# The last branch's gates of a token mixer in pairs, as block products of seven instead of eight

## The chip, the cores and the metric

The kernel runs on one core of one Trainium2 chip. The metric is the device time of one execution in microseconds (us). PE is TensorE, the matrix engine; DVE is VectorE, ACT ScalarE, POOL GpSimd, and SP the engine whose queue issues all DMAs here. `before.py` took a median of 2324.22 us in 3 runs.

## The reference

Two layers, each with a feed-forward block, a mixer and a second feed-forward block, over 512 tokens of width 1024, all in float32. In the mixer the change touches the merge of three branches:

```python
proj = h @ w_in                      # 1024 -> 7184 columns, the last 3072 are gate logits
...
conv_out = conformer_conv(conv_in, ...)   # GLU, causal depthwise conv, LayerNorm over 512, swish
...
branches = jnp.stack([sb_out, conv_out, gla_out], axis=2)      # each 512 x 512
branch_d = jnp.einsum('bsgw,gwd->bsgd', branches, w_branch)    # each to width 1024
gates = jax.nn.sigmoid(gate_logits.reshape(b, s, N_BRANCHES, D_MODEL))
merged = jnp.sum(gates * branch_d, axis=2)
return merged @ w_out
```

## The kernel before

Activations lie with channels on the 128 partitions and the 512 tokens along the free dimension. A float32 product is made of three products in a reduced format: each operand is split into a high half (`whi`, `xh`: a cast on ACT) and a low half (`wlo`, `xl`: the value less its cast, on DVE), and PE sums high x high, high x low and low x high. The normalised input of a layer part is the pair `xh`, `xl`, 8 tiles of 128 channels each.

The feed-forward blocks compute gate and up columns of 128 together, in *block products* (`block_tiles`): the product of a 2 x 2 arrangement of weights (halves of the 1024 inputs, two column tiles) with a 2 x 2 arrangement of activations (halves of inputs, halves of tokens) takes 7 smaller products instead of 8, of sums of blocks. Such a unit has 7 products of 12 matmuls of 256 columns, into three PSUM banks A, B and C. The sums of the activation blocks (T1 to T4, `Forms`) are made once per block, those of the weight blocks per unit by `prepare`, on DVE; ACT copies partial results out of the banks (`taken`), DVE combines them (`summed`).

The mixer, function `mixer`, computes its gates in `gates(g, src, done)`, for one branch g at a time: for each of 8 column tiles d a gate product `gate` of 24 matmuls of 512 columns (L66, called from `mm_cols`), a sigmoid on ACT, a branch product `pb` of 12 matmuls with the split branch output, and the multiply of both on DVE (L1245) and the addition to `acc[d]` on POOL (L1246). The order of the branches is attention (g = 0), linear attention (g = 2), convolution (g = 1), the last. While the gates of branch 2 run, DVE finishes the convolution's taps and the layer norm: `ln_tokens(i)` transposes 128 tokens (`ct`), takes mean and variance and writes `yn[i]`; `ln_back(i)` transposes back into four banks `cb0` to `cb3`, one per channel tile, where each `yn[i]` fills a quarter. After u_ = 5 the four tiles are scaled, put through the swish (L1377 to L1379) and split (`brh`, `brl`), all before the last branch begins.

The output projection, `Down`, is a block product again over `acc[0]` to `acc[3]`; `acc[4]` to `acc[7]`, block rows 4 to 7 of `w_out`, come last as plain products (banks oC, oD, oB, oA). `Down.run` calls `late`, which loads the next two norm rows (`g`). Then the residual `x_sb` is added.

What sets the order: PE's instructions stand in the order of the code; operations marked `pinned` too; all others are moved by the framework's scheduler on their engine. Every engine takes its queue in order, so what waits holds up what stands behind it. Pools hand out buffers: the raw weight tiles have 3 of two 512 KB halves, `whi` and `wlo` 5 each, `g` 2, PSUM 2 banks in "pa" and 6 in "pb".

Of the kernel before, what the change touches and what calls it, by code (L numbers as in the profile page):

```python
# [13 lines left out]
P = 128  # L14
# [27 lines left out]
def kernel(  # L42
# [19 lines left out]
    sm = ctx.enter_context(tc.tile_pool(name="sm", bufs=4))  # L62
    psp = ctx.enter_context(tc.tile_pool(name="psp", bufs=1, space=PSUM))
# [335 lines left out]
    class Forms:  # L399
# [26 lines left out]

        def finish(self, n):
# [23 lines left out]
    def block_tiles(w0, w1, fs, forms, hid, between):  # L451
# [4 lines left out]
        silu = lambda o, i: pin(nc.scalar.activation(o, i, AF.Silu))  # L456
# [3 lines left out]
        n = 7 * len(fs)  # L460
        raw, banks, cps, ring = {}, {}, {}, {}

        def load(u):
            r = wp.tile([P, 5, 512], F32, tag="raw", name="raw", bufs=3)
            for w, q0 in ((w0, 0), (w1, 1)):
                for j in range(2):
                    nc.sync.dma_start(r[:, q0 + 2 * j].rearrange("p (k c) -> p k c", c=P),
                                      w[j * 512:(j + 1) * 512, fs[u] * P:(fs[u] + 1) * P]
                                      .rearrange("(k p) c -> p k c", p=P))
            raw[u] = r  # L470
# [46 lines left out]
        def parts(u):  # L517
            cp = cps[u]
            return [cp[:, x * 256:(x + 1) * 256] for x in range(4)], hid[fs[u]], banks[u]

        def taken(g):

            u, j = divmod(g, 7)
            (p1, p7, u2, u4), h, (A, B, C) = parts(u)
            if j == 0:
                copy(p1, A[:, H0])
            if j == 1:
                copy(p7, C[:, H0])
            if j == 2:
                copy(u2, A[:, H0])  # L530
            if j == 4:
                copy(u4, A[:, H0])
            if j == 6:
                silu(h[:, H0], h[:, H0])
                silu(h[:, H1], A[:, H0])

        def summed(g):

            u, j = divmod(g, 7)
            (p1, p7, u2, u4), h, (A, B, C) = parts(u)  # L540
            if j == 3:
                add(h[:, H0], B[:, H0], p1)
            if j == 5:
                sub(u2, C[:, H0], u2)
                sub(u4, p7, u4)
            if j == 6:
                tt(h, cps[u][:, 512:1024], h, ALU.mult)

        for g in range(-AHEAD, n + 1):
            between(g)  # L550
            f = g + AHEAD
            if f % 7 == 0 and f < n:
                if f == 0:
                    load(0)
                if f // 7 + 1 < len(fs):
                    load(f // 7 + 1)
# [14 lines left out]
    class Down:  # L571
# [66 lines left out]
        def sums(self, p):  # L638
# [162 lines left out]
    def ffn(wg, wu, wd, weights, forms, arrive, finish, upcoming, early, late, begin):  # L801
# [72 lines left out]
        block_tiles(wg, wu, fs, forms, hid, between)  # L874
# [4 lines left out]
    def mixer(l, wv, arrive, finish, upcoming, early, late):  # L879
# [24 lines left out]

        cw = mp.tile([P, 4, NR], F32, tag="cw", name="cw")
# [270 lines left out]
        for h in range(HEADS):  # L1176
# [9 lines left out]
            att_values(h, ws)  # L1186
        next(decay[0])
# [13 lines left out]
        def gate_weights(g, d):  # L1201
            return load_cols(W, C_GATE + g * D + d * P)

        def gate_branch(g, d, src, wb, w):
# [5 lines left out]
            wh, wl = wb  # L1210
# [5 lines left out]
            return pb, sg  # L1216
# [13 lines left out]
        def gates(g, src, done):  # L1230

            early_ = done is not None
            following = gate_weights(g, 0) if early_ else None
            for d in range(0, KC, 2):
                wb = load_branch(g, d)
                for dd in (d, d + 1):
                    w = following if early_ else gate_weights(g, dd)
                    if early_ and dd + 1 < KC:
                        following = gate_weights(g, dd + 1)
                    pb, sg = gate_branch(g, dd, src, wb[dd - d], w)  # L1240
# [6 lines left out]
                    if done is not None:  # L1247
                        done(dd)
                    yield

        sb_gates = gates(0, branch_split(sbT, "s"), None)
# [82 lines left out]
        gla_gates = gates(2, branch_split(glaT, "t"), None)  # L1334


        cb = []
# [16 lines left out]
        def ln_back(i):  # L1354
            if not cb:
                cb.extend(bank(f"cb{c}") for c in range(4))
            for c in range(4):
                transpose(cb[c][:, i * P:(i + 1) * P], yn[i][:, c * P:(c + 1) * P], ident)

        for u_ in range(KC):  # L1360
            next(gla_gates)
            conv_taps(10)
            if u_ == 3:
                ln_tokens(0)
                ln_tokens(1)
            if u_ == 4:
                ln_back(0)
                ln_back(1)
                ln_tokens(2)
                ln_tokens(3)  # L1370
            if u_ == 5:
                ln_back(2)
                ln_back(3)
                for c in range(4):
                    g_, b_ = cw[:, c, TAPS + 1:TAPS + 2], cw[:, c, TAPS + 2:TAPS + 3]
                    s_ = slot("cs", tag="s")
                    nc.scalar.activation(s_, cb[c], AF.Sigmoid, scale=g_, bias=b_)  # L1377
                    nc.vector.tensor_scalar(ys[c], cb[c], g_, b_, op0=ALU.mult, op1=ALU.add)
                    nc.vector.tensor_tensor(ys[c], ys[c], s_, op=ALU.mult)  # L1379
                cv = branch_split(ys, "s")  # L1380
# [3 lines left out]
        down.pairs()  # L1384

        def merge(d):
            for n in range(2):
                down.sum_tokens(d, n)
            if d == KC - 2:
                for n in range(3):  # L1390
                    down.ahead()
# [23 lines left out]
    for idx, (l, s) in enumerate(subs):  # L1415
        norms = []

        def late():
            norms.append(load_g(norm_post[l, s]))
            if idx + 1 < len(subs):  # L1420
# [61 lines left out]
```

## Time and profile before

| | |
|---|---|
| three runs | 2323.63, 2324.22, 2324.99 us |
| the profiled execution | 2321.75 us, of which the span of its instructions 2320.0 us |
| granted PE clock, mean | 0.999 |
| busy in the span | PE 99%, DVE 81%, ACT 53%, POOL 8% |
| DMA | 269 MB, 116 GB/s in the mean |
| gates and branch products on the chain that ended last | PE gate 11%, PE pb 6% of the span |

Views of the profile are the page with its groups of instructions, the list of who waited for whom, the chain of work that ended last in order of time, timelines of one engine, and busy times by stretch. A row of a timeline has start, length, engine, line, operation, output and inputs, number, and in brackets the idle time before it with its releaser. Matmuls are pipelined: the length of one is longer than the distance to the next.

### The profile page before, as it was taken

The numbers are of one execution on the slowest core, as the hardware profiler recorded it, in microseconds if no ns is written. First come the engines' busy times: TensorE is split into PE (matmuls) and PEld (weight loads), VectorE is DVE, ScalarE is ACT, GpSimd is POOL, SyncE is SP. The second block draws the span as 40 slices with busy tenths as digits, with TensorE's granted clock in tenths as the row PEclk, the third lists the DMA queues.
The fourth block names the chain that finished last, engine by engine and source line by source line (L and its number), as shares of the span: only waits on it lengthen the run. The fifth ranks groups of instructions, "written<-read, shape, count | busy, mean of one in ns | idle before, by whom it ended". The sixth has DMA issues, their size and how long they took to land.

```text
span 2320.0 us, 35537 instructions
## 1 busy us (share of the span) xinstructions
PE 2296.1 (99%) x13664; PEld 2031.0 (88%) x13664; DVE 1884.6 (81%) x2819; ACT 1240.6 (53%) x2414; POOL 177.2 (8%) x277
## 2 busy tenths in 40 slices
PE   8999999999999999999999999999999999999998
PEld 7999888887888889998889998888878888899987
DVE  7888987859965688889888889878599647888897
ACT  5555656644323565556555566566433225566664
POOL 0000001201021200000000000012010212000000
PEclk9999999999999999999999999999999999999999
DMA  5333643131333423336433336432313324333363
GB/s 174 100 101 110 229 153 102 55 103 49 110 91 106 140 73 103 99 109 235 147 87 97 108 110 235 150 88 62 97 55 105 96 91 136 91 98 104 114 222 109
DMA packets 336219, 269.49 MB, mean 116 GB/s; under 512 B 13130, under 2 KB 285548, under 8 KB 336048
## 3 DMA queue, kind: packets, MB, share of 16 engines
q1 hardware_dynamic: 336048, 267.21, 38.0%
q8 instruction: 107, 1.75, 0.3%
q14 instruction: 64, 0.52, 0.1%
HBM read 265.07 MB, written 2.10 MB: 115 GB/s over the span
## 4 chain that ended last, share of the span: by engine, by line
PE 96%; DVE 2%; ACT 1%; issue 0%; DMA 0%; POOL 0%; SPq 0%; DVEq 0%; POOLq 0%; ACTq 0%
PE A L66 19%; PE gate L66 11%; PE oA L66 10%; PE C L66 9%; PE oC L66 6%; PE pb L66 6%; PE B L66 5%; PE oB L66 3%; PE pf L66 3%; PE gr L66 2%; PE pa L66 2%; PE q L66 2%; PE gv L66 2%; PE pv L66 2%; PE pgl L66 2%; PE k L66 2%
## 5 line engine op out<-in xcount | busy, mean ns | idle before, releaser
L457 DVE TENSOR_TENSOR wlo<-raw,whi 128x1024 fp32r<-128x1024 f32 (+1 forms) x304 | 331.1, 1089 | 106.9 <-ACT whi L455 106.1
L455 ACT CAST whi<-raw 128x512 fp32r<-128x512 f32 x532 | 315.3, 620 | 164.7 <-DVE raw L457 164.7
L115 ACT CAST whi<-raw 128x1024 fp32r<-128x1024 f32 (+1 forms) x162 | 168.1, 1044 | 329.8 <-PE gate L66 143.6
L116 DVE TENSOR_TENSOR wlo<-raw,whi 128x1024 fp32r<-128x1024 f32 (+1 forms) x162 | 203.4, 1265 | 137.3 <-ACT whi L115 133.0
L457 DVE TENSOR_TENSOR raw<-raw 128x512 f32<-128x512 f32 x304 | 209.2, 688 | 5.7
L66 PE MATMUL A<-xh,whi 128*128 128x256 f32 x608 | 172.5, 284 | 0.0
L66 PE MATMUL A<-xh,wlo 128*128 128x256 f32 x608 | 172.0, 283 | 0.0
L66 PE MATMUL A<-xl,whi 128*128 128x256 f32 x608 | 172.0, 283 | 0.0
L1055 DVE SCALAR_TENSOR_TENSOR y<-u,cw,y 128x511 f32<-128x511 f32 (+14 forms) x240 | 166.7, 755 | 0.0
L686 DVE TENSOR_TENSOR wlo<-raw,whi 128x1024 fp32r<-128x1024 f32 x122 | 148.8, 1220 | 17.8 <-ACT whi L683 17.5
L683 ACT CAST whi<-raw 128x1024 fp32r<-128x1024 f32 x122 | 128.4, 1052 | 63.8 <-issue 20.8
L66 PE MATMUL gate<-xh,whi 128*128 128x512 f32 x384 | 151.3, 394 | 0.0
L66 PE MATMUL gate<-xh,wlo 128*128 128x512 f32 x384 | 149.8, 390 | 1.3 <-DVE wlo L116 1.3
L66 PE MATMUL gate<-xl,whi 128*128 128x512 f32 x384 | 149.6, 390 | 0.0
L66 PE MATMUL oA<-whi,dl 128*128 128x512 f32 x352 | 137.0, 389 | 0.0
L66 PE MATMUL oA<-whi,dh 128*128 128x512 f32 x352 | 137.0, 389 | 0.0
L66 PE MATMUL oA<-wlo,dh 128*128 128x512 f32 x352 | 136.9, 389 | 0.0
L268 POOL TENSOR_TENSOR rs<-ms,mhalf 128x1 f32<-128x1 f32 x44 | 25.1, 576 | 1415.2 <-DVE ms L266 1415.2
L455 ACT COPY cp<-A 128x256 f32<-128x256 f32 x228 | 84.4, 370 | 66.5 <-PE A L66 65.6
L66 PEld LDWEIGHTS A<-xl,whi 128*128 128x128 f32 x608 | 116.6, 192 | 0.2
L66 PEld LDWEIGHTS A<-xh,whi 128*128 128x128 f32 x608 | 116.5, 192 | 0.2
L66 PEld LDWEIGHTS A<-xh,wlo 128*128 128x128 f32 x608 | 116.5, 192 | 0.0
(330 smaller groups left out, 6947.4 us busy)
## 6 DMA issues: line engine op xcount, KB each, us to landing
raw<-in_ffn_w_down_dram SPq DMA_DIRECT2D x152, 512.0 KB, 4.5
raw<-in_w_in_dram SPq DMA_DIRECT2D x108, 512.0 KB, 4.7
raw<-in_ffn_w_gate_dram SPq DMA_DIRECT2D x168, 256.0 KB, 3.4
raw<-in_ffn_w_up_dram SPq DMA_DIRECT2D x168, 256.0 KB, 4.5
raw<-in_w_branch_dram SPq DMA_DIRECT2D x24, 512.0 KB, 4.8
raw<-in_w_out_dram SPq DMA_DIRECT2D x24, 512.0 KB, 4.9
g<-in_norm_pre_dram SPq DMA_DIRECT2D x6, 512.0 KB, 6.8
g<-in_norm_post_dram SPq DMA_DIRECT2D x6, 512.0 KB, 5.8
```

The source lines that it names most:

```text
L66: tc.keep_in_program_order(nc.tensor.matmul(*a, **k))
L115: pin(nc.scalar.copy(hi, src))
L116: pin(nc.vector.tensor_tensor(lo, src, hi.bitcast(F32), op=ALU.subtract))
L268: nc.gpsimd.tensor_tensor(self.rs, ms, mhalf[:, 0:1], op=ALU.pow)
L455: copy = lambda o, i: pin(nc.scalar.copy(o, i))
L457: tt = lambda o, a, b, op: pin(nc.vector.tensor_tensor(o, a, b, op=op))
L683: pinned(nc.scalar.copy(hi, src))
L686: pinned(nc.vector.tensor_tensor(lo, src, hi.bitcast(F32), op=ALU.subtract))
L1055: nc.vector.scalar_tensor_tensor(y[:, back:], u[:, :S - back], cw[:, c, j:j + 1], y[:, back:], op0=ALU.mult, op1=ALU.add)
```

## The change

The gates of the last branch (g = 1) are computed in pairs (d, d + 1) as block products, by the same `block_tiles` as the feed-forward part: 4 units of 7 products of 12 matmuls of 256 columns in place of 8 products of 24 matmuls of 512. `block_tiles` now takes its weights, its target and what is done with the result as functions; a unit is prepared from 4 products ahead. After each unit follow the two branch products of its pair, in banks of "pa".

What the units need and what moves for it:
- The sums T1 to T4 are rebuilt from `xh` and `xl` (`Forms.rebuild`): T1 and T2 ahead of `conv_in(1)`, T3 and T4 behind the gates u_ = 3 and 4 of branch 2.
- Room for T1 and T2: the four tiles of the residual `x_sb`. So x is stored to DRAM at the mixer's start (`away`, 4 x 512 KB per layer) and loaded again in `Down.run`, between the norm rows (`back`).
- `ln_back(c)` now makes one channel tile c from all four `yn`, in steps: transposes ahead of product c of the first unit, swish one product later, split another one later, on pinned places. The last two gates of branch 2 run at g = -2 and g = 0 of the units' counter, that is ahead of the first product.
- The gates of branch 2 ask for their weights 2 column tiles ahead.
- For the last pair the addition to `acc` is on DVE, not POOL. `Down` keeps one of its weight sums in the place of `xh` and not in a second `g` buffer.

```diff
-    def block_tiles(w0, w1, fs, forms, hid, between):
+    def block_tiles(source, count, forms, target, result, between, ahead=AHEAD, wait=0):
...
             if j == 6:
-                silu(h[:, H0], h[:, H0])
-                silu(h[:, H1], A[:, H0])
+                results[u] = result(u, h, A[:, H0], cps[u][:, 512:1024])
+                next(results[u])
...
+        def rebuild(self, c, room_, second):
...
+            r11 = tokens(0, 0)
+            if not second:
+                r12 = tokens(0, 256)
+                tt(r12, r11, r12, ALU.subtract)
+                keep("T1", r12)
+                r22 = tokens(4, 256)
+                nc.vector.scalar_tensor_tensor(r22, r12, -1.0, r22, op0=ALU.mult, op1=ALU.subtract)
+                keep("T2", r22)
+                return
+            t2 = whole(*room_("T2", c))
+            tt(r11, t2, r11, ALU.add)
+            keep("T3", r11)
+            r21 = tokens(4, 0)
+            tt(r21, t2, r21, ALU.add)
+            keep("T4", r21)
...
-                    self.apart = [gp.tile([P, D], F32, tag="g", name="kept") for n in range(2)]
+                    self.apart = [gp.tile([P, D], F32, tag="g", name="kept")]
+                elif self.PER == 1 and j == 3:
+                    self.kept = room("xh", F32)
+                    self.apart.append(self.place(0))
...
+        for i in range(NT):
+            nc.sync.dma_start(away[i], x_sb[i])
...
+        for c in range(2):
+            mforms.rebuild(c, form_room, False)
         next(decay[0])
         conv_in(1)
...
+        def ln_back(c):
+            cb = bank("cb", "pa")
+            for i in range(NT):
+                transpose(cb[:, i * P:(i + 1) * P], yn[i][:, c * P:(c + 1) * P], ident)
+            yield
+            g_, b_ = cw[:, c, TAPS + 1:TAPS + 2], cw[:, c, TAPS + 2:TAPS + 3]
+            s_ = slot("cs", tag="s")
+            pinned(nc.scalar.activation(s_, cb, AF.Sigmoid, scale=g_, bias=b_))
+            pinned(nc.vector.tensor_scalar(ys[c], cb, g_, b_, op0=ALU.mult, op1=ALU.add))
+            pinned(nc.vector.tensor_tensor(ys[c], ys[c], s_, op=ALU.mult))
+            yield
+            held[0] = True
+            cv.extend(branch_split([ys[c]], "s"))
+            held[0] = False
...
+        def merged(u):
+            if u > 0:
+                for d in (2 * u - 2, 2 * u - 1):
+                    for n in range(2):
+                        down.sum_tokens(d, n)
+            for m, (ps, sg) in enumerate(zip(pbs[u], made[u])):
+                pinned(nc.vector.tensor_tensor(sg, ps, sg, op=ALU.mult))
+                d = 2 * u + m
+                (nc.vector if u == PAIRS - 1 else nc.gpsimd).tensor_tensor(acc[d], acc[d], sg, op=ALU.add)
+
+        def between(g):
+            u, j = divmod(g, 7)
+            if g in (-2, 0):
+                next(gla_gates)
+            if u == 0:
+                if j < 4:
+                    backs.append(ln_back(j))
+                for b in backs[-3:]:
+                    next(b, None)
+            if 0 <= u < PAIRS and j == 2:
+                held[0] = True
+                wbs[u] = load_branch(1, 2 * u)
+                held[0] = False
+            if u > 0 and j == 0:
+                branch_products(u - 1)
+            if u > 0 and j == 1:
+                merged(u - 1)
+            if g in (7 * PAIRS - 2, 7 * PAIRS - 1, 7 * PAIRS):
+                down.ahead()
+
+        block_tiles(source, PAIRS, mforms, target, sigmoids, between, 4, 4)
+        merged(PAIRS - 1)
+
+        def back():
+            for i in range(NT):
+                if i % 2 == 0:
+                    late(i // 2)
+                x_sb[i] = resid.tile([P, D], F32, tag=f"x{i}", name=f"x{i}")
+                pinned(nc.sync.dma_start(x_sb[i], away[i]))
-        for _ in gates(1, cv, merge):
-            pass
-        head = down.run(late, ("B0", "B1", "C0", "C1", "D0", "D1"))
+        head = down.run(back, ("B0", "B1", "C0", "C1", "D0", "D1"))
```

The order of the instructions at three places of the first layer (the numbers behind the names are those of the tiles). First DVE's queue from the scaling of the four channel tiles to the last low half, before: `cb0` to `cb3` are the banks of the way back, `cs` their sigmoid, `brl` the low half of the branch output, `gs` a gate multiplied with its branch product.

```order
L1378 TENSOR_SCALAR y_5463<-cb0_6900,cw_4134 128x512
L1378 TENSOR_SCALAR y_5548<-cb1_6901,cw_4134 128x512
L1379 TENSOR_TENSOR y_5463<-y_5463,cs_6995 128x512
L1379 TENSOR_TENSOR y_5548<-y_5548,cs_6999 128x512
L1378 TENSOR_SCALAR y_5647<-cb2_6902,cw_4134 128x512
L1378 TENSOR_SCALAR y_5743<-cb3_6903,cw_4134 128x512
L1379 TENSOR_TENSOR y_5647<-y_5647,cs_7003 128x512
L1379 TENSOR_TENSOR y_5743<-y_5743,cs_7007 128x512
L116 TENSOR_TENSOR brl_7012<-y_5463,brh_7011 128x512
L116 TENSOR_TENSOR wlo_7142<-raw_7134,whi_7141 128x1024
L116 TENSOR_TENSOR brl_7016<-y_5548,brh_7015 128x512
L116 TENSOR_TENSOR brl_7020<-y_5647,brh_7019 128x512
```

Now, from the last gate multiply of branch 2 (`gs_7148`) on; `raw_7063` holds the weights of the first unit, `raw_7170` those of the second, `wlo_7235` is the low half of the branch weights:

```order
L1315 TENSOR_TENSOR gs_7148<-pb_7150,gs_7148 128x512
L1432 TENSOR_SCALAR y_5473<-cb_7165,cw_4144 128x512
L1433 TENSOR_TENSOR y_5473<-y_5473,cs_7194 128x512
L493 TENSOR_TENSOR raw_7063<-raw_7063 128x512
L493 TENSOR_TENSOR wlo_7192<-raw_7063,whi_7191 128x2x512
L117 TENSOR_TENSOR brl_7221<-y_5473,brh_7220 128x512
L1432 TENSOR_SCALAR y_5586<-cb_7198,cw_4144 128x512
L1433 TENSOR_TENSOR y_5586<-y_5586,cs_7224 128x512
L117 TENSOR_TENSOR wlo_7235<-raw_7014,whi_7234 128x1024
L493 TENSOR_TENSOR wlo_7252<-raw_7063,whi_7251 128x512
L117 TENSOR_TENSOR brl_7256<-y_5586,brh_7255 128x512
```

and on to the last low half:

```order
L1432 TENSOR_SCALAR y_5685<-cb_7228,cw_4144 128x512
L1433 TENSOR_TENSOR y_5685<-y_5685,cs_7259 128x512
L493 TENSOR_TENSOR raw_7170<-raw_7170 128x512 x2
L493 TENSOR_TENSOR wlo_7252<-raw_7170,whi_7251 128x512
L117 TENSOR_TENSOR brl_7291<-y_5685,brh_7290 128x512
L1432 TENSOR_SCALAR y_5781<-cb_7263,cw_4144 128x512
L1433 TENSOR_TENSOR y_5781<-y_5781,cs_7294 128x512
L493 TENSOR_TENSOR gs_7203<-B_7176,cp_7178 128x256
L117 TENSOR_TENSOR brl_7315<-y_5781,brh_7314 128x512
```

The four tiles' scaling, multiply and split moved from one block behind the second gate from the end of branch 2 to places between the first unit's weight sums and weight halves, behind the multiply of branch 2's last gate.

Second, PE's queue where the last branch uses its first split tiles. Before, the first branch product of the last branch, behind a gate product of 24 matmuls:

```order
L66 MATMUL pb_7172<-brh_7011,whi_7136 128x512
L66 MATMUL pb_7172<-brl_7012,whi_7136 128x512
L66 MATMUL pb_7172<-brh_7011,wlo_7137 128x512
L66 MATMUL pb_7172<-brh_7015,whi_7136 128x512
L66 MATMUL pb_7172<-brl_7016,whi_7136 128x512
L66 MATMUL pb_7172<-brh_7015,wlo_7137 128x512
```

Now the last matmuls of the first branch product, which stands directly behind the first unit; `brl_7315` is the last of DVE's rows above:

```order
L67 MATMUL pb_7351<-brh_7290,whi_7234 128x512
L67 MATMUL pb_7351<-brl_7291,whi_7234 128x512
L67 MATMUL pb_7351<-brh_7290,wlo_7235 128x512
L67 MATMUL pb_7351<-brh_7314,whi_7234 128x512
L67 MATMUL pb_7351<-brl_7315,whi_7234 128x512
L67 MATMUL pb_7351<-brh_7314,wlo_7235 128x512
```

The branch product moved from behind a whole gate product to behind the unit in which its operands are made.

Third, SP's queue in the output projection, before:

```order
L127 DMA raw_7638<-in_w_out_dram 128x1024
L127 DMA raw_7693<-in_w_out_dram 128x1024
L193 DMA g_7689<-in_norm_post_dram 128x1024
L127 DMA raw_7693<-in_w_out_dram 128x1024
L193 DMA g_7691<-in_norm_pre_dram 128x1024
L127 DMA raw_7750<-in_w_out_dram 128x1024
L127 DMA raw_7750<-in_ffn2_w_gate_dram 128x2x256
```

and now:

```order
L128 DMA raw_7952<-in_w_out_dram 128x1024
L128 DMA raw_8015<-in_w_out_dram 128x1024
L194 DMA g_8003<-in_norm_post_dram 128x1024
L1519 DMA x0_8005<-away0_4136 128x1024
L1519 DMA x1_8007<-away1_4137 128x1024
L194 DMA g_8009<-in_norm_pre_dram 128x1024
L1519 DMA x2_8011<-away2_4138 128x1024
L1519 DMA x3_8013<-away3_4139 128x1024
L128 DMA raw_8015<-in_w_out_dram 128x1024
L128 DMA raw_8072<-in_w_out_dram 128x1024
L128 DMA raw_8072<-in_ffn2_w_gate_dram 128x2x256
```

The four loads of x stand between the norm rows, ahead of block rows 6 and 7 of `w_out` (the last two `w_out` rows in each list), which stood behind one norm row each.

More of the change, by code (lines that the diff above doesn't have):

```diff
@@ L518, in parts @@
             cp = cps[u]
-            return [cp[:, x * 256:(x + 1) * 256] for x in range(4)], hid[fs[u]], banks[u]
+            return [cp[:, x * 256:(x + 1) * 256] for x in range(4)], target(u), banks[u]
         def taken(g):
@@ L546, in summed @@
             if j == 6:
-                tt(h, cps[u][:, 512:1024], h, ALU.mult)
-        for g in range(-AHEAD, n + 1):
+                next(results[u], None)
+        for g in range(-ahead, n + 1):
             between(g)
[L551 to L556, printed above, removed]
+            f = g + ahead
+            if f == 0:
+                load(0)
+            if f < n and (f == wait if f < 7 else f % 7 == 0) and f // 7 + 1 < count:
+                load(f // 7 + 1)
             if 0 < g:
@@ L873, in ffn, with source, gated @@
         down = Down(wd, hid, 2, 8, (0, 1), (18, 19, 20, 21))
-        block_tiles(wg, wu, fs, forms, hid, between)
+        def source(u):
+            return (wg, fs[u] * P), (wu, fs[u] * P)
+        def gated(u, h, a, second):
+            pinned(nc.scalar.activation(h[:, H0], h[:, H0], AF.Silu))
+            pinned(nc.scalar.activation(h[:, H1], a, AF.Silu))
+            yield
+            pinned(nc.vector.tensor_tensor(h, second, h, op=ALU.mult))
+        block_tiles(source, len(fs), forms, lambda u: hid[fs[u]], gated, between)
         head = down.run(late)
@@ L903, in mixer @@
             vcat.append(row)
+        away = [scr.tile([P, D], F32, tag=f"away{i}", name=f"away{i}") for i in range(NT)]
+        for i in range(NT):
+            nc.sync.dma_start(away[i], x_sb[i])
         cw = mp.tile([P, 4, NR], F32, tag="cw", name="cw")
@@ L1186, in mixer, with form_room @@
             att_values(h, ws)
+        mforms = Forms()
+        rooms = {}
+        def form_room(n, c):
+            if n not in rooms and n in ("T1", "T2"):
+                j = 0 if n == "T1" else 2
+                rooms[n] = [resid.tile([P, D], F32R, tag=f"x{j + m}", name=f"{n}{m}")
+                            .rearrange("p (k t) -> p k t", k=4) for m in range(2)]
+            if n in rooms:
+                return [r[:, 2 * c:2 * c + 2] for r in rooms[n]]
+            return [slot(n, F32R, "t" if n == "T3" else "b").rearrange("p (k t) -> p k t", k=2) for m in range(2)]
+        for c in range(2):
+            mforms.rebuild(c, form_room, False)
         next(decay[0])
@@ L1228, in branch_split, with gates, ask @@
             return r
-        def gates(g, src, done):
-            early_ = done is not None
-            following = gate_weights(g, 0) if early_ else None
+        def gates(g, src, ahead=0):
+            wb, w = {}, {}
+            def ask(d):
+                if d < KC and d not in w:
+                    if d % 2 == 0:
+                        wb[d], wb[d + 1] = load_branch(g, d)
+                    w[d] = load_cols(W, C_GATE + g * D + d * P)
             for d in range(0, KC, 2):
-                wb = load_branch(g, d)
                 for dd in (d, d + 1):
[L1237 to L1240, printed above, removed]
+                    ask(dd)
+                    for n in range(ahead):
+                        ask(dd + 1 + n)
+                    pb, sg = gate_branch(src, w.pop(dd), wb.pop(dd))
                     if acc[dd] is None:
@@ L1246, in gates @@
                         nc.gpsimd.tensor_tensor(acc[dd], acc[dd], sg, op=ALU.add)
-                    if done is not None:
-                        done(dd)
                     yield
-        sb_gates = gates(0, branch_split(sbT, "s"), None)
+        sb_gates = gates(0, branch_split(sbT, "s"))
         gnB = mp.tile([P, 512], F32, tag="row", name="gnB")
@@ L1352, in ln_tokens @@
             nc.vector.tensor_scalar(yn[i], pt, mv[:, 0:1], rs, op0=ALU.subtract, op1=ALU.mult)
[L1354 to L1360, printed above, removed]
+        cv = []
+        def ln_back(c):
[8 more added lines that the diff above has]
+            pinned(nc.vector.tensor_tensor(ys[c], ys[c], s_, op=ALU.mult))
+            yield
+            held[0] = True
+            cv.extend(branch_split([ys[c]], "s"))
+            held[0] = False
+        for u_ in range(KC - 2):
             next(gla_gates)
@@ L1365, in mixer @@
                 ln_tokens(1)
+            if u_ in (3, 4):
+                mforms.rebuild(u_ - 3, form_room, True)
             if u_ == 4:
-                ln_back(0)
-                ln_back(1)
                 ln_tokens(2)
                 ln_tokens(3)
[L1371 to L1380, printed above, removed]
@@ L1383, in mixer, with source @@
         down = Down(w_out[l], acc, 0, 2, (), (4, 5, 6, 7))
         down.pairs()
[L1386 to L1391, printed above, removed]
-        for _ in gates(1, cv, merge):
-            pass
-        head = down.run(late, ("B0", "B1", "C0", "C1", "D0", "D1"))
+        PAIRS = KC // 2
+        wbs, pbs, made, backs = {}, {}, {}, []
+        def source(u):
+            c0 = C_GATE + D + 2 * u * P
+            return (W, c0), (W, c0 + P)
@@ new lines, in target, with sigmoids, branch_products @@
+        def target(u):
+            if u not in made:
+                made[u] = [slot("gs", tag="s")]
+            return made[u][0]
+        def sigmoids(u, h, a, second):
+            pinned(nc.scalar.activation(h[:, H0], h[:, H0], AF.Sigmoid))
+            pinned(nc.scalar.activation(h[:, H1], a, AF.Sigmoid))
+            pinned(nc.scalar.activation(second, second, AF.Sigmoid))
+            made[u].append(second)
+            yield
+        def branch_products(u):
+            pbs[u] = [bank("pb", "pa") for m in range(2)]
+            for ps, (wh, wl) in zip(pbs[u], wbs[u]):
+                branch_product(ps, cv, wh, wl)
@@ L1416, with late @@
         norms = []
-        def late():
-            norms.append(load_g(norm_post[l, s]))
-            if idx + 1 < len(subs):
+        def late(*which):
+            if not which or 0 in which:
+                norms.append(load_g(norm_post[l, s]))
+            if idx + 1 < len(subs) and (not which or 1 in which):
                 norms.append(load_g(norm_pre[subs[idx + 1][0], subs[idx + 1][1]]))
```

35 lines of the change are left out of this document (22 added, 13 removed).

## The prediction

> **What bounds the kernel now.** I read the page's busy times and its chain first, then what TensorE (PE) waited for, then the chain in order of time through the first layer's mixer, and last VectorE's (DVE) and ScalarE's (ACT) queues at the places that the change touches.
>
> ```profile
> PE 2296.1 (99%) x13664; PEld 2031.0 (88%) x13664; DVE 1884.6 (81%) x2819; ACT 1240.6 (53%) x2414; POOL 177.2 (8%) x277
> PE 96%; DVE 2%; ACT 1%; issue 0%; DMA 0%; POOL 0%; SPq 0%; DVEq 0%; POOLq 0%; ACTq 0%
> ```
>
> PE is busy in 2296 of 2320 us and carries 96% of the chain. Its waits, the whole list (us in total, times, longest):
>
> ```profile
> PE pt L71 <- DVE hn L223: 7.5, 1, 7.5
> PE pf L66 <- ACT xh L115: 4.3, 4, 2.0
> PE pt L71 <- DVE hn L290: 3.0, 3, 1.0
> PE gate L66 <- DVE wlo L116: 1.3, 2, 0.6
> PE pf L66 <- DVE xl L116: 0.8, 4, 0.2
> ```
>
> The gates' two waits, 1.3 us together, lie ahead of the last branch, which has none, as the chain shows next; so no wait can be removed there. The change can gain only by giving PE less to do, and can lose by making PE wait. What PE does, from the chain in order of time (start, length, what), with the last branch of both layers, the output projection behind it, and one block product of the feed-forward part for comparison:
>
> ```profile
> 687.18 0.87 PE cb L71 x8
> 697.11 0.87 PE cb L71 x8
> ...
> 714.32 5.44 PE gate L66 x24
> 719.76 2.72 PE pb L66 x12
> ...
> 776.88 2.72 PE pb L66 x12
> 779.60 2.72 PE oB L66 x12
> ...
> 866.78 1.44 PE A L66 x12
> 868.22 1.44 PE C L66 x12
> ...
> 1866.05 5.44 PE gate L66 x24
> ...
> 1931.33 2.72 PE oB L66 x12
> ```
>
> The reader sees a stage without a gap: from 714.32 to 779.60 are 65.28 us, which is 8 x (5.44 + 2.72), and from 1866.05 to 1931.33 again 65.28. One product of 512 columns costs 5.44 / 24 = 0.2267 us of PE, one of 256 columns 1.44 / 12 = 0.1200 us. The durations in the groups must not be used for this, since neighbours overlap:
>
> ```profile
> L66 PE MATMUL A<-xh,whi 128*128 128x256 f32 x608 | 172.5, 284 | 0.0
> L66 PE MATMUL gate<-xh,whi 128*128 128x512 f32 x384 | 151.3, 394 | 0.0
> ```
>
> **The change part by part.** *PE work.* A layer loses 8 gate products of 24 and gets 4 units of 7 block products of 12 short ones: 8 x 5.44 = 43.52 us becomes 28 x 1.44 = 40.32 us, so -3.20 us. Branch products (8 x 2.72) and the 16 transposes of the way back (2 x 0.87) stay, only placed otherwise. Two layers: -6.40 us, all of it on the path.
>
> The Trainium skill (TensorE: Matmul & The Clock Gate, Back-to-back issue gap) gives N / 2.4 + 2.5 ns between warm matmuls, 109 and 216 ns here. By it a pair of gates would save 48 x 0.2158 - 84 x 0.1092 = 1.19 us, 9.5 us in all, and the time would be an estimated 2314.7. The trace has 120 and 227 ns, 11 ns more in each case, and decides.
>
> *The first unit's DVE chain, the only stall that I find.* Before, the layer norm's way back was done long ahead of its use. Now one channel tile after another is transposed inside the first unit, and the branch product right behind this unit needs all four. DVE's rows of that time before:
>
> ```profile
> 700.28 1.52 DVE L1378 TENSOR_SCALAR y<-cb,cw 128x512 f32<-128x512 f32 x2
> 701.72 1.27 DVE L1379 TENSOR_TENSOR y<-y,cs 128x512 f32<-128x512 f32 x2
> 702.92 1.52 DVE L1378 TENSOR_SCALAR y<-cb,cw 128x512 f32<-128x512 f32 x2
> 705.56 0.68 DVE L116 TENSOR_TENSOR brl<-y,brh 128x512 fp32r<-128x512 f32 x1
> 706.17 1.21 DVE L116 TENSOR_TENSOR wlo<-raw,whi 128x1024 fp32r<-128x1024 f32 x1
> 707.30 1.88 DVE L116 TENSOR_TENSOR brl<-y,brh 128x512 fp32r<-128x512 f32 x3
> 714.42 0.69 DVE L1245 TENSOR_TENSOR gs<-pb,gs 128x512 f32<-128x512 f32 x1 [0.66 <-PE pb L66]
> 705.07 1.28 ACT L115 CAST brh<-y 128x512 fp32r<-128x512 f32 x2 [0.21 <-DVE y L1379]
> ```
>
> From start to start a scaled read of PSUM takes 1.44 / 2 = 0.72 us, a 512-wide operation 0.60 to 0.61, a 1024-wide one 1.13. In the new order DVE stands at the last gate multiply (gs) of the branch ahead until that product ends; this and 19 more operations come ahead of the low half (brl) of the last channel tile: 4 scaled reads, 13 of 512 (gs, 4 multiplies, 3 weight sums, 3 brl, 2 single low halves of weights), 2 of 1024 and one of 256 at about 0.3. That is 4 x 0.72 + 13 x 0.61 + 2 x 1.13 + 0.3 = 13.4 us, with the last brl at its full 0.68 14.0; two waits for ACT come to it (about 0.3 for a cast that stands behind a bank copy, 0.4 for the last high half, a cast of 0.6 us that can't start before its multiply has ended): 14.7 us. PE: without the two 0.87 us of transposes the branch ahead ends at 714.32 - 1.74 = 712.58, so DVE starts at 712.68 (its gs started 0.10 us behind PE's end) and ends at 727.4. PE does the transposes (1.74) and 7 x 1.44 = 10.08 and is at the branch product at 724.40; its 11th matmul, at 724.40 + 10 x 0.2267 = 726.67, needs that brl. It waits 0.7 us. The ends: nothing if the two ACT waits are overlapped; 2.3 us if each of the 21 takes its duration (0.08 more than the distance of starts). I take 0.7, because start-to-start distances held through the 8 us of rows above.
>
> *Later units.* A unit with its two branch products is 10.08 + 5.44 = 15.52 us of PE.
>
> ```profile
> 720.00:780.00 60.00, 60.00 (x266) 49.67 (x266) 25.04 (x29) 16.71 (x27) 9.06 (x7) 1.00 0.26 85
> 900.00:1050.00 150.00, 150.00 (x1251) 150.00 (x1250) 131.24 (x198) 89.73 (x197) 0.00 (x0) 1.00 0.36 106
> ```
>
> The columns are PE, weight load, DVE, ACT, POOL, granted clock (1.00), DMA share. In the feed-forward part the same unit keeps DVE busy 131 of 150 us, and PE waits for nothing. Here DVE has per unit 4 sums, 3.5 low halves of 1024, 3 of 256, plus one 1024 for branch weights, two multiplies and 4 halves of token sums: 2.4 + 4.0 + 1.0 + 1.1 + 1.2 + 1.4 = 11.1 of 15.52 us. Nothing.
>
> *Rebuilt operands.* 14 DVE operations of about 0.61 and 4 casts stand ahead of conv_in(1), as many behind the gates 3 and 4 of the branch ahead.
>
> ```profile
> 507.67 0.68 DVE L1096 COPY lrT<-pl 16x512 f32<-16x512 f32 x1
> 512.29 1.23 DVE L116 TENSOR_TENSOR wlo<-raw,whi 128x1024 fp32r<-128x1024 f32 x1 [3.94 <-ACT whi L115]
> 516.83 1.92 PE pal L66 x8
> 691.87 0.81 DVE L1352 TENSOR_SCALAR yn<-ct,mv,rsc 128x512 f32<-128x512 f32 x1 [0.15 <-POOL rsc L198]
> ```
>
> The first set delays lrT's copy by at most 14 x 0.61 = 8.5 us, to 516.9 at its end; but part of it goes into time in which DVE was idle, so I place that near 514, and pal needs it at 516.83. The second set pushes the last yn by 8.5 us, from 692.7 to about 701; the first transposes are at 712.58. Both hidden; without that idle time the first set would cost 0.1 us per layer.
>
> *Stores of x.* 4 x 512 KB leave at the start of the mixer, on SP in between the loads of the first projections' weights. The ends are nothing and the landing of one such load:
>
> ```profile
> raw<-in_w_in_dram SPq DMA_DIRECT2D x108, 512.0 KB, 4.7
> ```
>
> I take nothing: PE's value projection and the first query and key products run meanwhile, and in the list of waits no projection of the mixer waits for a weight. With that cover gone it would be the 4.7 us per layer.
>
> *Loads of x, the tail.* With T the start of oB, SP reaches the post-norm row at T + 2.1, and behind it now stand x0, x1, the pre-norm row, x2, x3, and only then block row 6 of w_out, which stood directly behind the post-norm row before.
>
> ```profile
> 781.72 0.33 SPq L193 DMA_DIRECT2D g<-in_norm_post_dram  x1
> 782.09 0.43 SPq L127 DMA_DIRECT2D raw<-in_w_out_dram  x1
> 780.00:790.00 10.00, 10.00 (x46) 8.29 (x45) 10.00 (x16) 7.76 (x13) 7.56 (x1) 1.00 0.84 307
> 798.00 1.05 ACT L683 CAST whi<-raw 128x1024 fp32r<-128x1024 f32 x1
> 791.77 0.76 DVE L685 TENSOR_TENSOR dl<-acc,dh 128x256 fp32r<-128x256 f32 x2 [1.18 <-POOL acc L1246]
> ```
>
> These are 7 x 0.524 = 3.67 MB. At the 307 GB/s of that row they take 12.0 us, and row 6 is cast at 798.00, T + 18.4, so 16.3 us are there: hidden with 4 us to spare. Upper end: at half that rate 23.9 us, 7.6 us late per layer. POOL's last two sums move to DVE ahead of the tail (1.2 us); DVE there later waited 1.18 us for POOL's sum, which goes, so nothing. The g buffers: one is free earlier, no wait gained.
>
> **Sum.** Per layer -3.20 + 0.7 = -2.5 us, both -5.0. The profiled execution took 2321.75 us (span 2320.0), 0.1% under the median 2324.22, so its span would be 2315.0, and the median 2324.22 - 5.0 = 2319.2.
>
> **The rivals.**
> 1. *No stall*: ACT's waits overlap, or DVE runs ahead. -6.4 us, 2317.8. For it: only 0.7 us separate the two. Against it: the 20 rows stand in one queue behind one wait, with no idle time to give.
> 2. *A longer chain in the first unit*: each extra us there is an extra us per layer, since all of it ends in the branch product. At 2.3 us per layer the gain is 1.8, 2322.4. For it: ACT holds 17 rows in the same time, and the 20 steps hand over to it and back. Against: the short units of the feed-forward part have the same exchange without a wait.
> 3. *Slower: the loads of x hold up rows 6 and 7 of w_out.* It needs fewer than 225 GB/s to delay PE at all, and decides for a loss below 3.67 MB / (16.3 + 2.5) us = 195 GB/s; at 154 GB/s it costs 7.6 per layer, 2334.4. For it: that queue holds seven transfers of one size, two of them broadcast rows. Against: the row with 307 GB/s already holds both kinds.
> 4. *Slower: short products cost more than half of long ones.* Break-even is 48 x 0.2267 / 84 = 0.1295 us; the rows above say 0.1200. With the mean durations (284 against 394 ns) one would get 84 x 0.284 - 48 x 0.394 = +4.9 per pair, 2364. The chain excludes it. The Trainium skill (TensorE: Matmul & The Clock Gate, Back-to-back issue gap) also states 81 ns for N = 128 and 131 for N = 512 in streams with weight loads; a straight line between gives an estimated 98 for 256, by which a pair would lose 1.9 us. The trace has neither number.
> 5. *More than the rows say*: if a short product cost just half of a long one, 0.1133, a pair would save 10.88 / 8 = 1.36 us, 10.9 in all, 2313.3. Nothing in the trace runs at that rate.
>
> **How the numbers follow.** The forecast (a stall of 0.3 to 1.1 us per layer) gets 46%, rival 1 17%, rival 2 24%, rival 3 10%, rivals 4 and 5 1% each, other losses 1%. A measurement of this kernel tells about 0.2%, 4.65 us, from no change; the gain passes it while the stall stays under 0.87 us per layer: rivals 1 and 5 and two thirds of the forecast, 0.17 + 0.01 + 0.31 = 0.49. Slower is 0.12 (rivals 3 and 4, other losses), the rest 0.39 is within. The range goes from 2317.4 (rival 1 with 0.4 less than its bound) to 2325.0, past the end of rival 2, and leaves out most of rivals 3 and 4.
>
> **What would show it.** In the changed profile: the pieces A, C, B of 1.44 us between the branch products; the first piece pb of each layer longer by about 0.7 us, with a wait for DVE brl; oB about 2.5 us earlier against the gates of the branch ahead; no wait of a projection piece for w_out. Wrong would be: a wait of A or C for wlo in the units, or one of oC behind 800 for a transfer.

## The result, and the profile after

The changed kernel takes 2332.96 us (median of 6 runs, 2331.59 to 2333.67) against 2323.74 us before (6 runs, 2322.89 to 2324.99): a ratio of 1.004, interval 1.0029 to 1.0051. It is 9.2 us slower where 5.0 us less had been forecast, and outside the range of 2317.4 to 2325.0. The profiled execution has a span of 2331.2 us. Its page, busy times and shares of the chain:

```profile
PE 2298.5 (99%) x13952; PEld 2041.0 (88%) x13952; DVE 1955.9 (84%) x2951; ACT 1275.4 (55%) x2510; POOL 165.7 (7%) x273
PE 94%; DVE 3%; ACT 1%; issue 1%; DMA 0%; POOL 0%; SPq 0%; DVEq 0%; POOLq 0%; ACTq 0%
```

PE still looks full, and though it has 6.4 us less to do its busy time is 2.4 us longer than before (2296.1). Its share of the chain fell by two points, and DVE's rose by one. The list of PE's waits names what is new (us in total, times, longest):

```profile
PE A L67 <- ACT cp L492: 8.4, 4, 4.0
PE cb L72 <- DVE y L1432: 0.7, 2, 0.4
```

The chain in order of time through the last branch, first layer and then second (start, length, what):

```profile
714.26 0.45 PE cb L72 x4
...
727.95 0.70 DVE y L1433
...
728.68 0.62 ACT brh L116
729.30 0.28 ACT cp L492
...
729.62 2.68 PE A L67 x12
732.30 6.04 PE pb L67 x24
738.34 1.43 PE A L67 x12
...
784.96 2.72 PE oB L67 x12
...
1870.63 0.45 PE cb L72 x4
...
1886.00 2.08 PE A L67 x12
1888.08 6.65 PE pb L67 x24
...
1941.35 2.72 PE oB L67 x12
```

From the first transposes (714.26) to the output projection (784.96) are 70.70 us, in the second layer 70.72. The work in it is 1.74 us of transposes and 4 x (10.08 + 5.44) = 62.08, together 63.82: 6.88 us per layer are stalls, where 0.7 had been forecast. They all lie in the first unit; from 738.34 on three units take 46.62 us, 15.54 each, as counted. So the stage, 65.28 us before, costs 70.70 - 1.74 - 65.28 = 3.7 us more per layer instead of 2.5 less.

What PE stood for is seen in the queues of the first unit (start, length, engine, line, what, in brackets the idle time ahead and what ended it):

```profile
714.36 0.69 DVE L1315 TENSOR_TENSOR gs<-pb,gs 128x512 f32<-128x512 f32 x1 [4.44 <-PE pb L67]
727.95 0.69 DVE L1433 TENSOR_TENSOR y<-y,cs 128x512 f32<-128x512 f32 x1
729.33 0.69 DVE L117 TENSOR_TENSOR brl<-y,brh 128x512 fp32r<-128x512 f32 x1 [0.35 <-ACT brh L116]
728.68 0.62 ACT L116 CAST brh<-y 128x512 fp32r<-128x512 f32 x1 [1.99 <-DVE y L1433]
729.20 0.36 ACT L492 COPY cp<-A 128x256 f32<-128x256 f32 x1
729.62 0.39 PE L67 MATMUL A<-xh,whi 128*128 128x256 f32 x1 [3.96 <-ACT cp L492]
```

DVE works almost without a pause from 714.36 to the last multiply of the way back, which ends at 728.64. ACT waits for it with the cast `brh`, and behind this cast, in the same queue, stands the copy of bank A that PE's seventh product needs before it may write there. So PE stands from 725.6 to 729.6. And when it goes on it is slow: 12 short products take 2.68 us instead of 1.44, the 24 long ones 6.04 instead of 5.44, 1.84 us more, in the second layer 2.08 and 6.65, 1.85 more. The view by stretches (us; busy time of PE, weight load, DVE, ACT, POOL; then the granted clock, the DMA share and GB/s) says why:

```profile
725.60:729.60 4.00, 0.06 (x1) 0.00 (x0) 3.61 (x7) 1.96 (x4) 0.00 (x0) 1.00 1.05 316
729.60:732.30 2.70, 2.68 (x13) 2.68 (x14) 2.02 (x3) 1.46 (x3) 0.00 (x0) 0.56 0.24 79
732.30:735.00 2.70, 2.70 (x11) 2.11 (x11) 1.49 (x4) 1.52 (x3) 0.00 (x0) 0.80 0.00 0
```

After the 4 us of idling PE's clock is granted at half from 729.95 to 733.36, for 3.41 us. The page counts the slow matmuls as busy: they are 3.7 of the 8.8 us by which the busy time lies above the 2289.7 that 6.4 us less would have given. Of the rest about 4 us lie outside the two stages.

### The profile page after: what moved, and what is told of

Read it like the earlier page. It is cut to its first block, busy times and chain, and to the rows that moved or that the text cites. A ratio compares the mean times of both kernels' runs of the same rounds, so it can differ in the third digit from the quotient of the medians.

```text
span 2331.2 us, 36377 instructions
## 1 busy us (share of the span) xinstructions
PE 2298.5 (99%) x13952; PEld 2041.0 (88%) x13952; DVE 1955.9 (84%) x2951; ACT 1275.4 (55%) x2510; POOL 165.7 (7%) x273
## 4 chain that ended last, share of the span: by engine, by line
PE 94%; DVE 3%; ACT 1%; issue 1%; DMA 0%; POOL 0%; SPq 0%; DVEq 0%; POOLq 0%; ACTq 0%
PE A L67 20%; PE C L67 10%; PE oA L67 10%; PE gate L67 8%; PE oC L67 6%; PE pb L67 6%; PE B L67 5%; PE oB L67 3%; PE pf L67 3%; PE gr L67 2%; PE pa L67 2%; PE q L67 2%; PE gv L67 2%; PE pv L67 2%; PE pgl L67 2%; PE k L67 2%
## 5 line engine op out<-in xcount | busy, mean ns | idle before, releaser
L493 DVE TENSOR_TENSOR wlo<-raw,whi 128x1024 fp32r<-128x1024 f32 (+1 forms) x336 | 366.1, 1090 | 124.3 <-ACT whi L492 123.4
L492 ACT CAST whi<-raw 128x512 fp32r<-128x512 f32 x588 | 349.2, 620 | 198.9 <-DVE raw L493 195.7
L116 ACT CAST whi<-raw 128x1024 fp32r<-128x1024 f32 (+2 forms) x146 | 151.2, 1043 | 225.7 <-PE gate L67 100.1
L493 DVE TENSOR_TENSOR raw<-raw 128x512 f32<-128x512 f32 x336 | 234.5, 698 | 5.9
L117 DVE TENSOR_TENSOR wlo<-raw,whi 128x1024 fp32r<-128x1024 f32 (+2 forms) x146 | 175.1, 1209 | 72.3 <-ACT whi L116 66.6
L67 PE MATMUL A<-xh,whi 128*128 128x256 f32 x672 | 191.4, 285 | 7.9 <-ACT cp L492 7.9
L67 PE MATMUL A<-xh,wlo 128*128 128x256 f32 x672 | 190.9, 284 | 0.0
L67 PE MATMUL gate<-xh,whi 128*128 128x512 f32 x256 | 101.3, 396 | 0.0
L67 PE MATMUL gate<-xh,wlo 128*128 128x512 f32 x256 | 100.0, 390 | 1.3 <-DVE wlo L117 1.3
L67 PE MATMUL gate<-xl,whi 128*128 128x512 f32 x256 | 99.8, 390 | 0.0
```

The source lines that it names most:

```text
L67: tc.keep_in_program_order(nc.tensor.matmul(*a, **k))
L116: pin(nc.scalar.copy(hi, src))
L117: pin(nc.vector.tensor_tensor(lo, src, hi.bitcast(F32), op=ALU.subtract))
L492: copy = lambda o, i: pin(nc.scalar.copy(o, i))
L493: tt = lambda o, a, b, op: pin(nc.vector.tensor_tensor(o, a, b, op=op))
```

## The experiments

The theory to be tested: the first unit's chain makes the whole loss, by a queue order (a bank copy behind a cast that waits for DVE) and by a second price, the clock. Against it stood: DVE is simply too full there, so that the wait only moves; ACT's own load; and the other parts of the change (rebuilt operands, stores and loads of x).

**The way back ahead of the last gate.** The transposes go to four banks, as before the change; sigmoids and multiplies stand ahead of the gate, the last casts and low halves just ahead of it.

```diff
+            if g == -2:
+                ln_transposes()
...
+                for c in (0, 1): next(backs[c]); next(backs[c])
+            if g == -1:
...
-            if u == 0:
-                if j < 4: backs.append(ln_back(j))
-                for b in backs[-3:]: next(b, None)
```

> The layer norm's way back (transposes, sigmoid, multiplies, casts, low halves) is put ahead of the last gate of the branch ahead, in four banks, as it was before; the block units stay. Theory A (the loss of the changed kernel is the first unit's chain: TensorE lost 6.2 us of waits and 0.6 us of slow branch products per layer there, 6.87 us against 11.82 + 5.44 us of work): both layers' 13.7 us go, 2333.0 - 13.7 = 2319.3. Rival B (the loss comes from the rebuilt operands, the stores and loads of x or the feed-forward stages): stays above 2330. Rival C (the way back ahead pushes the low halves of the second and third block product behind it on VectorE): a new wait of 1 to 2 us per layer on these, 2321 to 2323.

Measured: 2323.34 us, ratio to before 1.0000 (0.9991 to 1.0008). The loss of the changed kernel is gone, so it lay in this stage and not in what the edit left alone. But the gain did not come: PE still waits for a bank copy, 1.67 and 1.95 us. Its list of waits, and in the first layer ACT's cast and copy, DVE's weight sum and POOL's sum:

```profile
PE A L67 <- ACT cp L492: 3.6, 2, 1.9
```

```profile
726.35 0.62 ACT L492 CAST whi<-raw 128x512 fp32r<-128x512 f32 x1 [3.80 <-issue]
726.88 0.36 ACT L492 COPY cp<-A 128x256 f32<-128x256 f32 x1
723.89 2.38 DVE L493 TENSOR_TENSOR raw<-raw 128x512 f32<-128x512 f32 x2
720.59 5.14 POOL L1316 TENSOR_TENSOR acc<-acc,gs 128x512 f32<-128x512 f32 x1 [11.35 <-DVE gs L1315]
```

The same pattern one link further: the copy stands behind the cast of a weight sum of the next unit, and that sum ends only at 726.27 in DVE's queue (723.89 + 2.38), slowed by POOL's (the run with this sum on DVE, below, shows that). The forecast for this run missed it just as the prediction had missed the first.

**Only ACT's order: copies ahead of the channel tiles' casts.**

```diff
                 taken(g - 1)
+            if behind:
+                behind(g)
...
```

`behind` holds a channel tile's cast and its low half.

> Only ScalarE's order in the first unit is changed: the cast of a channel tile's high half stands behind the copy of a bank that stood behind it, so that the last copy of bank A no longer waits for VectorE's last multiply. VectorE's work stays the same. Theory A (TensorE's 4.0 us are a wait for that copy, which stood behind the cast, and the 1.85 us behind it are the clock at half after the wait): the copy comes after 726.1 instead of 729.2, TensorE waits 0.5 to 1.4 us and keeps its clock, and the last low half at 730.0 comes just in time for the branch product; 4.4 us per layer less, 2333.0 - 8.8 = 2324.2 (2322 to 2325). Rival B (VectorE's chain decides, the wait only moves to the branch product's eleventh product): waits of 4 us stay, 2330 to 2333. Rival C (the clock falls after a short wait too): 1.85 us per layer more than A, 2327.9.

Measured: 2326.89 us, ratio 1.0013 (1.0004 to 1.0021). Of the 9 us above before, 6 are gone by where ACT's casts stand, with the same work on both engines (the low halves on DVE move with their casts). Theory A had the right copy and the wrong size: the wait is 2.4 us in both layers, since the copy now stands behind the weight sum's cast, not 0.5 to 1.4. The clock fell in the first layer and stayed in the second, after waits of 2.41 and 2.42 us:

```profile
723.15:726.56 3.41, 1.00 (x9) 0.80 (x8) 3.34 (x6) 1.30 (x3) 0.00 (x0) 1.00 0.99 250
726.56:729.97 3.41, 3.41 (x13) 3.02 (x13) 2.73 (x6) 1.58 (x3) 0.00 (x0) 0.50 0.67 229
1876.85:1880.27 3.42, 1.58 (x14) 1.38 (x12) 3.35 (x6) 0.99 (x2) 0.00 (x0) 1.00 1.10 302
1880.27:1883.68 3.41, 2.83 (x18) 2.62 (x19) 3.38 (x7) 1.15 (x3) 0.00 (x0) 1.00 0.90 296
```

**Two of the four channel tiles ahead.**

```diff
+                for c in range(4):
+                    s = g - (-2, -2, 0, 0)[c]
...
```

> Two of the four channel tiles are taken back ahead of the last gate of the branch ahead, into VectorE's idle 4.4 us there, the other two at the first two products of the unit. Theory A (VectorE's chain in the first unit, 15.7 us without a pause, is too long by the 4 us that TensorE waits): it gets 3.9 us shorter, the last low half lands near 726, no wait above 0.5 us is left: 2319.3, up to 2321. Rival B (casts of ScalarE, not VectorE's length, hold the copies): waits of 2 to 4 us stay, 2326 to 2333.

Measured: 2327.83 us, ratio 1.0019 (1.0010 to 1.0028). DVE has only 2.7 us less to do in the unit (2 x (0.72 + 0.61); the two low halves stayed behind the gate's multiply), and a wait of 2.14 us stands now ahead of the fifth product, in both layers: two casts that wait for DVE's multiplies hold the copies of banks C and A behind them. In the second layer one of 1.07 us ahead of the seventh product comes to it.

```profile
722.60 0.62 PE L67 MATMUL A<-T,whi 128*128 128x256 f32 x2 [2.14 <-ACT cp L492]
```

Rival B held: what counts is what stands ahead of a copy, not DVE's length alone.

**The stores and loads of x in the kernel before.**

```diff
+        for i in range(NT):
+            nc.sync.dma_start(away[i], x_sb[i])
...
+        head = down.run(back, ("B0", "B1", "C0", "C1", "D0", "D1"))
```

> The kernel before, with nothing but the four stores of x at the start of the mixer and its four loads in the output projection. Theory A (these cost nothing, as forecast; the 3.4 us that the changed kernel waited more for w_down in the four feed-forward stages, 7.0 against 3.6 us on VectorE, do not come from them): 2323.7, within 1 us, w_down waits near 3.6 us. Rival B (the added traffic or the memory behind it moves the w_down loads): about 3 us more, 2327, w_down waits near 7. Rival C (they hold up w_in or w_out): a wait of a projection for a weight, up to 7.6 us per layer, 2331 to 2339.

Measured: 2324.58 us against 2324.05, ratio 1.0002 (0.9994 to 1.0011). They cost nothing that can be measured, and no projection waits for a weight. But DVE's waits for w_down are 6.7 us here too; a second profile of the kernel before is compared with it.

> The kernel before once more, for a second profile. In its first profile VectorE waited 3.6 us for loads of w_down, in all five others since 6.4 to 7.0, and that profiled execution was 2.4 us under the median of its kernel. Theory A (the first one was an execution with early loads; the change and the stores of x have no part in it): 6 to 7 us of these waits, a span near 2322.5. Rival B (the scratch memory or the stores of x move these loads): 3.6 us again, a span near 2320.

DVE's waits for w_down in the changed kernel, in the kernel before with stores of x, and in the second profile of the kernel before:

```profile
DVE xh L679 <- DMA raw<-in_ffn_w_down_dram: 7.0, 10, 1.4
```

```profile
DVE xh L646 <- DMA raw<-in_ffn_w_down_dram: 6.7, 8, 1.9
```

```profile
DVE xh L645 <- DMA raw<-in_ffn_w_down_dram: 4.6, 7, 1.1
```

It took 2323.43 us with 4.6 us of these waits. That lies between the theories. Executions do differ by as much: in the first feed-forward block, which stands ahead of every store of x, these waits are 0.8 to 2.7 us in the changed kernel and the seven runs built on it, and none of their edits touches this block. Whether the scratch memory adds to it stays open; by the run with the stores it is at most 0.11% (2.6 us).

**The way back ahead, and the ninth product's cast behind the copy.**

```diff
...
-            if f < n:
+            if f < n and f != hold:
+                if f - 1 == hold:
+                    prepare(hold)
                 prepare(f)
...
```

`hold` is 8, the ninth product counted from 0; the way back stands as in the first run.

> As the run with the way back ahead, and in each first unit ScalarE's cast for the ninth block product (which waits for a weight sum of VectorE) is put behind the copy of bank A that stood behind it. Theory A (what was left of the loss, 1.67 and 1.95 us of waiting for that copy, is again a copy queued behind a cast that waits for VectorE): the waits go, 3.6 us, and the piece behind them takes 1.44 instead of 1.70 us: 2323.3 - 4.1 = 2319.2, 0.2% under the kernel before, and no wait of A for a copy. Rival B (VectorE is too full in the first unit, the wait moves to a low half or a later copy): 2322 to 2324.

Measured: 2319.76 us, ratio 0.9983 (0.9974 to 0.9992), 4.1 us faster than before and 13.2 under the changed kernel. The chain of the first unit has no gap:

```profile
716.11 1.43 PE A L67 x12
...
724.74 1.44 PE A L67 x12
726.18 5.47 PE pb L67 x24
```

The four units take 62.18 us (oB starts at 778.29) against 65.28 before: the 3.20 us of fewer columns are real, less 0.1. A wait of 0.3 us of the output projection's second product for DVE's last sums, and other small ones, take part of it back.

**Inside the first unit, with both orders mended.** The two edits to ACT's order together (`behind` and `hold`), with the way back where the change has it.

> The changed kernel with its way back inside the first unit, but with both orders of ScalarE mended: the bank copies ahead of the channel tiles' casts, and the cast for the ninth product behind the last copy. Here the only wait left should be the one that the prediction had (the branch product's eleventh product for the last low half). Theory A: that low half lands at about 728.4 against 727.6 needed, 0.8 us, and 0.4 us for the last copy; no wait over 2 us and no half clock: 2326.9 - 2 x 1.2 - 1.8 = 2322.7. Rival B (VectorE's chain costs the same wherever the wait stands): 2326 to 2327.

Measured: 2325.97 us, ratio 1.0010 (1.0001 to 1.0019): rival B. No wait over 0.8 us, no half clock, and the one wait of my prediction is there (`pb` for `brl`, 0.29 us in each layer). But PE now stops four times per layer, twice of it in the second unit:

```profile
PE A L67 <- ACT cp L492: 2.6, 4, 0.8
PE C L67 <- DVE wlo L493: 1.0, 2, 0.5
PE pb L67 <- DVE brl L117: 0.6, 2, 0.3
```

```profile
714.00:730.00 16.00, 15.21 (x113) 13.83 (x112) 15.14 (x22) 9.43 (x18) 1.29 (x1) 1.00 0.45 128
730.00:746.00 16.00, 14.69 (x103) 13.46 (x102) 12.53 (x14) 8.09 (x17) 3.00 (x2) 1.00 0.26 68
```

DVE is busy 15.14 of the first 16 us and passes its lateness on to the second unit. So order was one half of the loss, and DVE's load in this unit the other.

**The last sum of the branch ahead on DVE.**

```diff
-                        nc.gpsimd.tensor_tensor(acc[dd], acc[dd], sg, op=ALU.add)
+                        (nc.vector if ahead and dd == KC - 1 else nc.gpsimd).tensor_tensor(...)
...
```

> As the first of these, and the sum of the last gate of the branch ahead is done by VectorE instead of GpSimd. In the run with the way back ahead this sum took 5.14 us on GpSimd while VectorE was busy, and a weight sum of VectorE that fell into it took 1.67 instead of 0.68 us. Theory A (the two engines hold each other up): the two weight sums behind it take 1.29 us instead of 2.38, VectorE gains 1.0 us and pays 0.6 for the sum; the time stays within 1 us of the first of these, 2319. Rival B (the long sum comes from its operands): the weight sums still take 2.38.

Measured: 2319.41 us, ratio 0.9983 (0.9974 to 0.9992), the same as the run with the ninth product's cast behind the copy, to which this edit is added. The pair of weight sums behind it takes 1.41 us instead of 2.38; theory A holds.

```profile
723.24 1.41 DVE L493 TENSOR_TENSOR raw<-raw 128x512 f32<-128x512 f32 x2
```

**Without the low halves of the way back.**

```diff
-            cv.extend(branch_split([ys[c]], "s"))
+            sh = slot("brh", F32R, "s")
+            pinned(nc.scalar.copy(sh, ys[c]))
+            cv.append((sh, sh))
```

> The changed kernel without the four low halves (brl) of the way back in the first unit: VectorE has 2.4 us less to do there, and the branch products read the high half in the place of the low one, with as many products. ScalarE's order stays. Theory A (the bank copy waits behind the last cast, which waits for VectorE's chain): three of the four stood ahead of the last multiply, so the copy comes 1.8 us earlier and TensorE waits 2.1 to 2.3 us instead of 3.96, twice 1.8 less: 2329.4, and 2325.7 if the clock then stays up in both layers. Rival B (ScalarE's own load sets the copy): the wait stays near 4 us, 2332 to 2333.

This kernel leaves the low halves out of the branch products, which read the high half twice. Measured: 2329.62 us, ratio 1.0021 (1.0011 to 1.0030), forecast 2329.4. The copy:

```profile
726.56 0.62 ACT L1436 CAST brh<-y 128x512 fp32r<-128x512 f32 x1 [1.44 <-DVE y L1433]
727.08 0.36 ACT L492 COPY cp<-A 128x256 f32<-128x256 f32 x1
727.50 0.58 PE L67 MATMUL A<-xh,whi 128*128 128x256 f32 x1 [2.77 <-ACT cp L492]
```

Counted from the first transpose (713.73 here, 714.10 in the changed kernel) it comes at 13.35 instead of 15.10 us, 1.75 earlier for 1.8 forecast: taking work from DVE moves ACT's copy one to one, so DVE's chain sets it and ACT's own load does not. The wait is 2.77 us and not 2.1 to 2.3, because PE too comes to it earlier, by 0.56 us: its stop of 0.35 us for `y` is gone. And in the first layer the half clock lasts twice as long and costs 3.1 us. So the time came out nearer the forecast than its parts did. The clock fell in both layers after 2.77 us:

```profile
727.50:730.00 2.50, 2.50 (x11) 2.50 (x12) 1.89 (x3) 1.39 (x3) 0.00 (x0) 0.50 0.77 257
730.00:732.00 2.00, 2.00 (x8) 1.61 (x7) 0.09 (x1) 1.41 (x3) 0.00 (x0) 0.50 0.00 1
```

## Why the prediction was wrong

**PE work: right.** The units run at 1.44 us per product, and with no stall in them the stage is 3.1 us per layer shorter.

**The first unit's chain: the step that failed.** Its place was right, and DVE's row of work nearly so: from the gate's multiply to the end of the last low half 15.66 us (714.36 to 730.02) for 14.7 forecast. Wrong was the sentence that PE "is at the branch product" and waits there for `brl` at "its 11th matmul". It set the last block product (1.44 us) and ten branch products (2.27) as cover beside DVE's chain. But a product needs, besides its operands, a bank whose partial sum has been copied out, and that copy stood in ACT's queue behind a cast of the same chain. So those 3.7 us lay behind the chain. I followed DVE's results to PE and never ACT's queue to PE's banks. That gives the 4 us in place of 0.7; two smaller waits of the same kind (0.35 for `y`, 0.24 for another copy) come to it, each with some tenths around it that a wait's row does not count.

**A price that the prediction did not have:** 1.85 us per layer of half clock behind the wait. Together 6.88 - 0.7 = 6.2 us per layer more than forecast, 12.4 for both, of the 9.2 + 5.0 = 14.2 us between forecast and result. The other 1.8 us lie outside the two stages. There the changed kernel's profile is 3.8 us longer, and 2.0 of these go off, since the profiled execution before was that much under its median. They are not shown one by one: the output projection's oA takes 0.17 and 0.29 us more, and the loads of w_down vary from one execution to the next.

**Rival 2** (a longer chain in the first unit) named the place and the steps that hand over between DVE and ACT, but let all of it end in the branch product and was sized at 2.3 us; its reason against, that the feed-forward units make the same exchange without a wait, fails because DVE has 4 x (0.72 + 0.61 + 0.61) = 7.8 us of way back on top there.

**Later units, rebuilt operands, stores and loads of x: right.** Units two to four take 15.54 us for 15.52; the last `yn` started at 700.55 for "about 701", with no wait behind it; the stores cost nothing; no projection of PE waits for w_out (rival 3), though DVE waits 3.1 us for its loads. Rivals 4 and 5 would show in the pieces of 1.44, which are as the rows said.

**The size of the whole** came out in the end, 2319.8 for 2319.2, but only in a kernel with other orders; it does not vindicate the forecast.

## What to carry to other kernels

For every matmul ask two questions: when are its operands ready, and who copies out the bank it writes, on which queue, behind what. Work of PE counts as cover for a chain only as far as it stands ahead of the first instruction that waits for anything in that chain, the copies behind casts included. When a chain is to be moved into a busy stage, look first where its engine now stands idle: here DVE waited 4.4 us for the gate just ahead, and the same work put there, with one cast moved, turned +9 us into -4.

## What the runs showed of the hardware

**PE's clock after a wait.** It fell to half after waits of 3.96 and 3.97 us (changed kernel) and twice after 2.77; after 2.41 and 2.42, and after 2.14 twice (two tiles ahead), it fell in the first layer alone; after 1.67 and 1.95 it stayed. Each fall cost 1.8 us, once 3.1. What decides is not the length of the wait alone. In all eleven traces the granted clock changes only at points that lie whole multiples of 3.41 us apart. If the traces are cut at these points, from the first one on (at 15 to 18 us), half clock follows full clock behind each of the 16 stretches with at most 1.42 us of busy PE, and behind none of the over 7000 with 1.58 us or more. The run with the copies first has both cases: in the first layer its wait lies in one such stretch, in the second it is shared by two (the four rows shown with it; in each PE's busy time stands first behind the length, the clock third from the end). The Trainium skill (TensorE: Matmul & The Clock Gate, Part 1) says that the clock is gated to half after at least one idle window of about 3.4 us, and that the windows run freely. That the clock falls or stays after the same wait agrees with free windows; the falls after 2.1 to 2.8 us are shorter waits than its figure, and the measurement decides.

**DVE and POOL hold each other up.** POOL's sum of 512 columns took 1.29 us in the last branch before the change, where DVE was mostly idle, and 5.14 beside a busy one (way back ahead); two DVE sums next to it took 2.38 instead of 1.41. The Trainium skill (SBUF — State Buffer, SBUF: two separate sides) has it as an exclusive lock of a shared port pair, held for a whole instruction. These numbers agree with two engines that block each other, and the run with the sum on DVE, where the two sums take 1.41 us, shows that POOL's sum slowed them; how long the lock is held no run here shows.
